# Swapping the last two block products of each fast up pair in a gated decoder block

## The chip, the cores and the metric

The kernel runs on one core of a Trainium2 chip. Its time is the device time of one execution in microseconds (us). The core has five engines with a queue of instructions each: TensorE (PE in the profile; its weight loads are listed apart as PEld), VectorE (DVE), ScalarE (ACT), GpSimd (POOL) and SyncE (SP). They work side by side and meet at semaphores. An engine takes its own instructions in the order in which they stand in its queue.

## The reference, cut to what matters

One layer of a hybrid decoder runs on 512 positions with 16 learned positions ahead of them, in float32: a normalised input goes through gated linear attention and through a pooling branch, both are merged and added to the residual, and then comes the gated MLP, where the change is. Everything is held transposed, with channels on the partitions.

```
hn = rmsnorm(h, norm2_g)
up = causal_dwconv(hn @ w_up, conv_w, conv_b)     # w_up: 1024 x 5632, conv over 3 positions
a, bv = split(up, 2)                              # 2816 channels each
h = h + (silu(a) * bv) @ w_down                   # w_down: 2816 x 1024
out = rmsnorm(h, final_norm_g)[:, 16:]
```

## The kernel before, in words

A float32 product is made of three matmuls on the format float32r: each operand is split into a high part and a remainder, and high*high, high*remainder and remainder*high are summed in PSUM.

The MLP's 2816 hidden channels are 22 tiles of 128. A step `("up", i)` makes tile i of both `a` and `bv`, so it is called a pair here; a step `("down", part, m)` makes two of the eight output tiles from a part of the hidden tiles. `seq` lists them: ups 0 to 9, two downs (n = 10, 11), up 10 (n = 12), two downs, ups 11 to 15 (n = 15 to 19), two downs, up 16 (n = 22), two downs, ups 17 to 21 (n = 25 to 29), and eight downs from n = 30. Ups 0 to 3 are done plainly by `up_plain`. The 18 ups from 4 on go through `up_fast`: the pair is seen as a product of 2x2 blocks (two halves of the contraction, two halves of the positions, `a` and `bv`), and seven block products replace eight, with sums of weight blocks and of input blocks made beforehand. Each call of `seven` is one block product: 12 matmuls of 258 columns on TensorE.

The seven products go to four PSUM banks `x`, `y`, `q` and `v`. Bank `x` gets three products on top of each other and is copied out by ScalarE after each (lines 788, 793, 797, into the blocks z11, z12 and z21 of `z`); bank `q` gets two (copied out after the first by line 790, and added to z12 by VectorE after the second, line 801); `y` and `v` get one each. A further product may only be written into a bank once the copy of its last state has been read: the fourth product waits for line 788, and the last one in `x` waits for line 793.

What each pair reads, and who makes it:

- `own[n]`, tiles `gh` and `gl` (high part and remainder of three weight blocks; two buffers each), is made by `make_own`: ScalarE writes minus the high part into `gl` (line 654), then GpSimd issues three DMAs (two for a down) that add the weights from DRAM to it (line 656), so that the remainder is left, and ScalarE copies the high part to `gh` (line 657):

```
act.activation(lo, src, AF.Copy, scale=-1.0)
for piece in pieces:
    pool.dma_start(lo[piece], dram[piece], accum_op=ALU.add)
act.activation(hi, src, AF.Copy)
```

- `sums[n]`, tiles `sh_<n>a`, `sl_<n>a`, `sh_<n>b`, `sl_<n>b` (two buffers each, shared by a and b), is made by `make_sums`: four VectorE additions within the loaded weights `raw` (line 692), in place and so only after `gh` has read them, then the two splits (ScalarE, line 249, and VectorE, line 250). The b sums of the next pair go into the buffer that this pair's b sums hold until its sixth and seventh product have read them.
- The pair ends with `prepare(n, behind)`: it fetches further weights and calls `make_own(n + 2)`, whose ScalarE instructions are queued behind the instruction `behind`, which is the copy of line 797.

After a pair, `conv` works on the pair three before it: the convolution, the gate and the split of the gated tile (lines 814 to 821, ScalarE and VectorE).

The order of the text isn't the order on an engine. The framework's scheduler gives each engine its order when the program is built: it takes what it reckons ready, by its own estimate of times. So in pair 4 TensorE runs 8 matmuls of the fifth product, all 12 of the fourth, and then the other 4 of the fifth, though the text has the fourth first. On the chip the order within an engine is fixed.

Of the kernel before, what the change touches and what calls it, by code (L numbers as in the profile page):

```python
# [13 lines left out]
ALU = mybir.AluOpType  # L14
# [54 lines left out]
def hybrid_block(ctx: ExitStack, tc: tile.TileContext, xt, g1d, wts, wup, wdown, wglr, wgk, vecs, out):  # L69
    nc = tc.nc  # L70
    act, dve, pool, pe, sp = nc.scalar, nc.vector, nc.gpsimd, nc.tensor, nc.sync
# [556 lines left out]
    def bank(name):  # L628
        return bankp.tile([P, 512], F32, tag="bank", name=name)
# [67 lines left out]
    def weights(n):  # L697
        make_sums(n)
        make_sums(n + 1)
        return (own[n], *sums.get(n, ()))  # L700

    def prepare(n, behind=None):
        fetch(n + 2)
        fetch(n + 3)
        if behind is None:
            make_own(n + 2)
        else:
            with tc.issue_after(behind.ins):
                make_own(n + 2)
# [4 lines left out]
    def pairtile(name, dt=F32):  # L714
        return flat(name, unitp, dt)
# [34 lines left out]
    direct, crossed = [], []  # L750
# [20 lines left out]
    def seven(acc, w, block, x, at, first=True):  # L771
        for k in range(4):
            for e, (a, b) in enumerate(((0, 0), (0, 1), (1, 0))):
                pe.matmul(  # L774
                    acc[:, 0:HN], w[a][:, block, k], x[k][b][:, at],
                    start=first and k == 0 and e == 0, stop=k == 3 and e == 2,
                    skip_group_check=not first,
                )

    def up_fast(n, i):  # L780
        g, sa, sb = weights(n)
        z = pairtile(f"z{i}").rearrange("p (a b) -> p a b", a=2)
        z11, z12 = (z[:, 0, a:b] for a, b in HALF)
        z21, z22 = (z[:, 1, a:b] for a, b in HALF)
        x, y, q, v_ = (bank(f"{c}{i}") for c in "xyqv")
        n_ = slice(0, HN)
        seven(x, g, 2, direct, 2)
        act.activation(z11, x[:, n_], AF.Copy)
        seven(q, sa, 0, crossed, 1)
        act.activation(z22, q[:, n_], AF.Copy)  # L790
        seven(v_, g, 0, crossed, 3)
        seven(x, sa, 1, crossed, 2, False)
        act.activation(z12, x[:, n_], AF.Copy)
        seven(y, g, 1, direct, 0)
        dve.tensor_tensor(z11, y[:, n_], z11, ALU.add)
        seven(x, sb, 1, crossed, 0, False)
        behind = act.activation(z21, x[:, n_], AF.Copy, scale=-1.0)
        dve.tensor_tensor(z22, z21, z22, ALU.subtract)
        dve.tensor_tensor(z21, v_[:, n_], z21, ALU.add)
        seven(q, sb, 0, direct, 1, False)  # L800
        dve.tensor_tensor(z12, q[:, n_], z12, ALU.add)
        prepare(n, behind)
        zs[i] = z

# [29 lines left out]
    for n, job in enumerate(seq):  # L834
        if job[0] == "up":
            i = job[1]
            (up_plain if i < PLAIN else up_fast)(n, i)
            if i >= LAG:
                conv(i - LAG)
            if i == FF - 1:  # L840
                for k in range(FF - LAG, FF):
                    conv(k)
                table(LOG_EXP, silus[-1])
        elif job[1] < 3:
            (w,) = weights(n)
            for c in range(2):
                acc = bank(f"pd{n}_{c}")
                down(acc, w, c, job[1], (0, 512))
                h = h2[2 * job[2] + c][:, META:]
                dve.tensor_tensor(h, acc, h, ALU.add)  # L850
            prepare(n)
# [113 lines left out]
```

## Time and profile before

| what | us |
|---|---|
| median of 3 runs | 855.51 |
| lowest and highest run | 855.21, 858.98 |
| the profiled execution, its own time | 854.07 |
| span of its instructions | 852.4 |

The profile is of one execution; its span leaves out 1.7 us around the program. Views used below: the page's list of busy time per engine; the waits (who waited for whom); the chain of work that ended last (each row: start, length, what; followed back from the last instruction); the timeline (start, length, engine, line, operation, out<-in, and in brackets the idle time before it with what ended it). Tile names lose their numbers in most places, so `x`, `q`, `gl`, `gh`, `raw` stand for those of all pairs; `z` of line 793 is the copy of z12, `z` of line 797 that of z21.

### The profile page before, as it was taken

How to read it: one execution, taken by the hardware profiler on the slowest of the kernel's cores; microseconds unless marked ns; L12 is line 12 of the kernel's file. 1: busy time of each engine (PE TensorE's matmuls, PEld its weight loads, DVE VectorE, ACT ScalarE, POOL GpSimd, SP SyncE). 2: the span in 40 equal slices, each digit the busy share in tenths (PEclk: the TensorE clock that was granted, in tenths of full speed). 3: DMA queues.
4: the chain of work that ended last, by engine and by line, in shares of the span. 5: the costliest groups of instructions: out<-in, count | busy, mean ns of one | idle time of the engine just before them, and what ended most of it. 6: DMA issues, size and time to landing. Idle time of an engine off the chain costs nothing.

```text
span 852.4 us, 15085 instructions
## 1 busy us (share of the span) xinstructions
PE 827.7 (97%) x6357; PEld 795.8 (93%) x6357; DVE 526.2 (62%) x817; ACT 440.4 (52%) x622; POOL 144.2 (17%) x149
## 2 busy tenths in 40 slices
PE   8999999999999999999999999999999999999993
PEld 6999999999999999999999999998899987999772
DVE  6677335379756433355555488995569844897425
ACT  7287134266234212353263357885568854777562
POOL 3000000001740000000022122221222222221241
PEclk9999999999999999999999999999999999999997
DMA  7423221122323322362275074867977777877763
GB/s 240 128 64 110 76 75 50 33 77 66 118 81 99 100 86 89 100 198 83 92 248 173 1 172 100 194 154 198 216 167 161 183 177 184 185 162 174 152 92 102
DMA packets 35780, 109.96 MB, mean 129 GB/s; under 512 B 4000, under 2 KB 6816, under 8 KB 32896
## 3 DMA queue, kind: packets, MB, share of 16 engines
q1 hardware_dynamic: 20368, 79.10, 27.8%
q0 software_dynamic: 14112, 28.84, 20.5%
q8 instruction: 50, 0.82, 0.4%
q10 hardware_dynamic: 1232, 1.05, 0.4%
q14 instruction: 18, 0.15, 0.0%
HBM read 106.88 MB, written 2.10 MB: 128 GB/s over the span
## 4 chain that ended last, share of the span: by engine, by line
PE 79%; DMA 7%; ACT 6%; DVE 5%; issue 2%; SPq 0%; DVEq 0%; POOL 0%; ACTq 0%
PE pd L829 9%; PE pu L150 5%; PE pv L150 5%; PE po L150 5%; PE pb L150 5%; PE pgb L150 5%; PE pga L150 5%; PE pr L150 5%; PE pa L150 5%; PE x L774 5%; DMA gl<-in_wdown_dram 5%; PE pup L733 4%; PE q L774 4%; PE pq L150 3%; DVE raw L692 2%
## 5 line engine op out<-in xcount | busy, mean ns | idle before, releaser
L133 ACT ACTIVATE whi<-wraw 128x1024 fp32r<-128x1024 f32 (+2 forms) x78 | 78.9, 1014 | 202.5 <-PE pa L150 36.4
L134 DVE TENSOR_TENSOR wlo<-wraw,whi 128x1024 fp32r<-128x1024 f32 (+2 forms) x78 | 94.8, 1218 | 13.0 <-ACT whi L133 7.2
L656 POOL DMA_DIRECT2D gl<-in_wup_dram x66 | 59.1, 1219 | 226.7 <-ACT gl L654 215.4
L829 PE MATMUL pd<-g,gh 128*128 128x512 f32 (+1 forms) x304 | 93.2, 388 | 0.0
L657 ACT ACTIVATE gh<-raw 128x1536 fp32r<-128x1536 f32 (+1 forms) x38 | 54.5, 1435 | 47.1 <-issue 26.1
L829 PEld LDWEIGHTS pd<-g,gh 128*128 128x128 f32 x304 | 56.5, 188 | 11.9
L829 PE MATMUL pd<-g,gl 128*128 128x512 f32 (+1 forms) x152 | 59.3, 390 | 3.2 <-DMA gl<-in_wdown_dram 3.2
L692 DVE TENSOR_TENSOR raw<-raw 128x512 f32<-128x512 f32 x72 | 49.5, 688 | 15.6 <-ACT gl L654 12.0
L654 ACT ACTIVATE gl<-raw 128x1536 fp32r<-128x1536 f32 (+1 forms) x38 | 54.4, 1431 | 0.8 <-DMA raw<-in_wup_dram 0.5
L535 POOL TENSOR_TENSOR pt<-u 128x1028 f32<-128x1028 f32 (+3 forms) x4 | 14.0, 3498 | 191.9 <-ACT whi L133 179.0
L656 POOL DMA_DIRECT2D gl<-in_wdown_dram x32 | 28.1, 1040 | 106.1 <-ACT gl L654 94.7
L850 DVE TENSOR_TENSOR h<-pd,h 128x512 f32<-128x512 f32 x24 | 16.5, 689 | 42.9 <-PE pd L829 42.8
L829 PEld LDWEIGHTS pd<-g,gl 128*128 128x128 f32 x152 | 28.6, 188 | 10.8 <-DMA gl<-in_wdown_dram 3.8
L815 DVE SCALAR_TENSOR_TENSOR cv<-z,vec,cv 128x512 f32<-128x512 f32 x44 | 32.7, 748 | 9.1 <-ACT cv L814 9.0
L814 ACT ACTIVATE cv<-z,vec 128x512 f32<-128x512 f32 x44 | 34.0, 812 | 0.0
L816 DVE SCALAR_TENSOR_TENSOR cv<-z,vec,cv 128x512 f32<-128x512 f32 x44 | 32.5, 747 | 0.2
L150 PE MATMUL pr<-xh,whi 128*128 128x258 f32 (+1 forms) x128 | 26.1, 285 | 0.0
L150 PE MATMUL pv<-xh,wlo 128*128 128x264 f32 x128 | 26.0, 285 | 0.0
L150 PE MATMUL pu<-xh,wlo 128*128 128x258 f32 (+3 forms) x128 | 25.9, 284 | 0.0
L150 PE MATMUL pv<-xl,whi 128*128 128x264 f32 x128 | 25.9, 284 | 0.0
L150 PE MATMUL pu<-xh,whi 128*128 128x258 f32 (+3 forms) x128 | 25.9, 284 | 0.0
L150 PE MATMUL pu<-xl,whi 128*128 128x258 f32 (+3 forms) x128 | 25.9, 284 | 0.0
(821 smaller groups left out, 2756.2 us busy)
## 6 DMA issues: line engine op xcount, KB each, us to landing
wraw<-in_wts_dram SPq DMA_DIRECT2D x72, 512.0 KB, 3.6
raw<-in_wup_dram SPq DMA_DIRECT2D x22, 1024.0 KB, 8.0
gl<-in_wup_dram POOLq DMA_DIRECT2D x66, 256.0 KB, 7.4
raw<-in_wdown_dram SPq DMA_DIRECT2D x12, 768.0 KB, 7.9
gl<-in_wdown_dram POOLq DMA_DIRECT2D x24, 384.0 KB, 8.1
h<-in_xt_dram SPq DMA_DIRECT2D x4, 514.0 KB, 6.0
raw<-in_wdown_dram SPq DMA_DIRECT2D x4, 512.0 KB, 4.8
gl<-in_wdown_dram POOLq DMA_DIRECT2D x8, 256.0 KB, 5.7
```

The costliest lines, as they stand in the source:

```text
L133: act.activation(hi[:, a:b], t[:, a:b], AF.Copy)
L134: dve.tensor_tensor(lo[:, a:b], t[:, a:b], f32(hi[:, a:b]), ALU.subtract)
L150: pe.matmul(acc[:, s, : b - a], w, x[:, a:b], start=(i == 0 and w is wh and x is xh), stop=(i == n - 1 and last),)
L654: act.activation(lo, src, AF.Copy, scale=-1.0)
L656: pool.dma_start(lo[piece], dram[piece], accum_op=ALU.add)
L657: act.activation(hi, src, AF.Copy)
L692: dve.tensor_tensor(raw[:, dst], raw[:, dst], raw[:, x], ALU.add)
L733: pe.matmul(acc[:, 0 : b - a], w[p], q[k][:, a:b], start=k == 0 and e == 0, stop=k == KT - 1 and e == 2,)
L774: pe.matmul(acc[:, 0:HN], w[a][:, block, k], x[k][b][:, at], start=first and k == 0 and e == 0, stop=k == 3 and e == 2, skip_group_check=n ...
L814: act.activation(cv, z[:, c, META:], AF.Identity, scale=v1("cw2", m), bias=v1("cb", m))
L815: dve.scalar_tensor_tensor(cv, z[:, c, META - 1 : L - 1], v1("cw1", m), cv, ALU.mult, ALU.add)
L829: pe.matmul(acc, w[p][:, c, k], gated[k0 + k][q][:, a:b], start=k == 0 and e == 0, stop=k == nk - 1 and e == 2,)
```

## The change

Within `up_fast` the sixth and seventh block products change places. Before, the sixth is the last one into bank `x` and the seventh the last one into bank `q`; after, `q` comes first. The VectorE addition that follows `q`'s product moves up with it. The copy of line 797, the two additions that use it, and `prepare`, whose work hangs behind that copy, keep their place behind `x`'s product and so come at the end.

```diff
         seven(y, g, 1, direct, 0)
         dve.tensor_tensor(z11, y[:, n_], z11, ALU.add)
+        seven(q, sb, 0, direct, 1, False)
+        dve.tensor_tensor(z12, q[:, n_], z12, ALU.add)
         seven(x, sb, 1, crossed, 0, False)
         behind = act.activation(z21, x[:, n_], AF.Copy, scale=-1.0)
         dve.tensor_tensor(z22, z21, z22, ALU.subtract)
         dve.tensor_tensor(z21, v_[:, n_], z21, ALU.add)
-        seven(q, sb, 0, direct, 1, False)
-        dve.tensor_tensor(z12, q[:, n_], z12, ALU.add)
         prepare(n, behind)
```

No instruction is added, removed or resized.

## The prediction

> **What bounds the kernel now.** I read the page's list of busy time first:
>
> ```profile
> span 852.4 us, 15085 instructions
> PE 827.7 (97%) x6357; PEld 795.8 (93%) x6357; DVE 526.2 (62%) x817; ACT 440.4 (52%) x622; POOL 144.2 (17%) x149
> ```
>
> TensorE is busy nearly throughout, and the change gives it the same matmuls. So it can only move the little time in which TensorE waits. The waits of TensorE and of its weight loads between 518 and 790 us come next (who waited for whom: us in total, times, longest):
>
> ```profile
> PEld pd L829 <- DMA gl<-in_wdown_dram: 3.8, 3, 2.1
> PEld x L774 <- ACT z L793: 2.7, 7, 0.4
> PE x L774 <- ACT z L793: 1.2, 6, 0.2
> ```
>
> Among the pairs one wait stands out: the sixth product, the last into bank `x`, waits for line 793's copy of z12. It happens in 7 of 18 pairs. The other row belongs to the downs. What a waiting pair costs is read from the chain of waits (start, length, what):
>
> ```profile
> 528.03 0.97 PE y L774 x8
> 529.00 1.46 PE x L774 x12
> 530.46 0.48 PE y L774 x4
> 530.93 1.72 PE x L774 x12
> ...
> 539.83 1.43 PE y L774 x12
> 541.26 1.45 PE x L774 x12
> ...
> 551.32 1.45 PE x L774 x12
> ...
> 585.46 8.29 DMA gl<-in_wdown_dram
> ...
> 593.79 7.88 PE pd L829 x33
> ...
> 636.17 1.64 PE x L774 x12
> ...
> 646.62 1.71 PE x L774 x12
> ...
> 657.14 1.73 PE x L774 x12
> ...
> 667.68 1.73 PE x L774 x12
> ...
> 733.49 1.65 PE x L774 x12
> ...
> 765.01 1.73 PE x L774 x12
> ```
>
> Without a wait a product takes 1.43 to 1.45 us, and from one sixth product to the next it is 551.32 - 541.26 = 10.06 us. With the wait it is 667.68 - 657.14 = 10.54 us. So a full wait costs 0.48 us. Six pairs have it (646.62 to 667.68, and three more, the last at 765.01). Two have a short one (636.17 and 733.49, 1.64 and 1.65 instead of 1.45: 0.2 us each), and pair 4 has 530.93 with 1.72 (0.27 us). Together 6 x 0.48 + 0.4 + 0.27 = 3.55 us.
>
> Why the copy is late stands in ScalarE's timeline of one such period:
>
> ```profile
> 655.76 1.06 ACT L249 ACTIVATE sh_18a<-raw 128x1024 fp32r<-128x1024 f32 x1 [0.84 <-DVE raw L692]
> 656.72 0.37 ACT L793 ACTIVATE z<-x 128x258 f32<-128x258 f32 x1
> 656.99 0.62 ACT L818 ACTIVATE cv<-cv 128x512 f32<-128x512 f32 x1
> 658.90 0.39 ACT L797 ACTIVATE z<-x 128x258 f32<-128x258 f32 x1 [1.29 <-PE x L774]
> 659.19 1.48 ACT L654 ACTIVATE gl<-raw 128x1536 fp32r<-128x1536 f32 x1
> 660.57 1.04 ACT L249 ACTIVATE sh_18b<-raw 128x1024 fp32r<-128x1024 f32 x1
> 661.51 1.48 ACT L657 ACTIVATE gh<-raw 128x1536 fp32r<-128x1536 f32 x1
> 662.89 0.62 ACT L249 ACTIVATE g<-cv 128x512 fp32r<-128x512 f32 x1
> 663.41 0.37 ACT L788 ACTIVATE z<-x 128x258 f32<-128x258 f32 x1
> ...
> 666.30 1.06 ACT L249 ACTIVATE sh_19a<-raw 128x1024 fp32r<-128x1024 f32 x1 [0.84 <-DVE raw L692]
> ```
>
> Line 793's copy stands behind sh_18a, and sh_18a waits for VectorE's additions in `raw`, which wait for `gh`, which stands behind sh_18b, `gl` and line 797's copy, which waits for the product that waited. That is a ring of 10.54 us, longer than TensorE's 10.06. In the earlier pairs the order is the other way round, and nothing waits:
>
> ```profile
> 559.98 0.39 ACT L793 ACTIVATE z<-x 128x258 f32<-128x258 f32 x1 [0.43 <-PE x L774]
> 561.25 1.06 ACT L249 ACTIVATE sh_8a<-raw 128x1024 fp32r<-128x1024 f32 x1 [0.88 <-DVE raw L692]
> ```
>
> **The change part by part.** Nothing is added or removed: 7 x 12 matmuls, four copies, four additions and the same DMAs per pair. The two products cost TensorE the same in either order (1.45 us each).
>
> *What goes.* Between the fourth product, which line 793 reads, and the last into `x` there is now `q`'s product as well as `y`'s. The copy has 1.45 us more, and the worst wait was 0.48. If line 793's copy is not put off by as much, all 3.55 us go.
>
> *What is moved: line 797's copy and all that hangs behind it.* It now waits for the end of the pair, 1.45 us later. Behind it on ScalarE stand `gl`, the b sums and `gh` of the rows above, and then line 788's copy for the next pair. The b sums alone lose nothing: their buffer comes free at the pair's end in both versions. I count from S, the start of the next pair's first product. A product's end in the chain lies 0.17 us after the next one's first matmul begins, and line 797's copy starts 0.03 us after that (667.68 + 1.73 = 669.41, the copy at 669.44): S + 0.20. By the rows above `gh` starts 2.61 us behind it (661.51 - 658.90), at S + 2.81, sh_a 4.79 us behind `gh` (655.76 less the `gh` of that period, one ring of 10.54 before 661.51), at S + 7.60, and line 788's copy 4.51 us behind line 797's, ending at S + 5.08. Who is late then:
>
> First, line 788's copy. The fourth product is due at S + 3 x 1.43 = S + 4.29 and needs it. It would be 0.8 us late. But the scheduler knows that, and pair 4 is the row nearest to it: there `gh` also came late, line 788's copy ran from 527.75 to 528.12, and TensorE was given 8 matmuls of `y` ahead of the fourth product and lost nothing.
>
> ```profile
> 525.86 1.47 ACT L657 ACTIVATE gh<-raw 128x1536 fp32r<-128x1536 f32 x1
> 527.24 0.61 ACT L249 ACTIVATE g<-cv 128x512 fp32r<-128x512 f32 x1
> 527.75 0.37 ACT L788 ACTIVATE z<-x 128x258 f32<-128x258 f32 x1
> ```
>
> I expect that in most pairs: with all of `y` ahead, the fourth product starts at S + 5.73 and the copy is done. The cost of an interleaved product, 1.46 instead of 1.43 (529.00), is 0.03 us x 13 pairs = 0.4 us. The bounds are 0 (an order of products without any cost) and 13 x 0.9 = 11.7 us (no reordering; 0.8 of waiting and the 0.1 that a first matmul after a wait took longer in the rows above). I take 0.4, because the only pair in this position shows it.
>
> Second, the DMAs into `gl`, issued by GpSimd after line 654. The tightest pair is number 9, whose weights are issued at 564.93 (with the landing times of its three: min, median, max); its third product reads the second of them:
>
> ```profile
> 564.93 2.65 POOL L656 DMA_DIRECT2D gl<-in_wup_dram  x3 [7.40 <-ACT gl L654]
> DMA to landing us min/median/max: 4.3/9.8/10.3
> ```
>
> ```profile
> 577.29 0.28 PE L774 MATMUL v<-xh,gl 128*128 128x258 f32 x1
> ```
>
> The second is issued at most 2.65 / 3 = 0.9 us after the first and takes at most 10.3, so it is there by 576.1, and the product that uses it starts at 577.29: 1.2 us of slack, at the worst. It turns into a wait of 0.3 us at most in this pair, and stays positive where the landing is 9.8. I take 0, with 0.3 us x 10 pairs (those whose `gl` is made two pairs earlier, within a row of pairs) = 3 us as the upper end.
>
> Third, the second down after a pair. Its `gl` is late already: pair 9's line 654 starts at 583.68, the DMA at 585.46 lands at 593.75, and the down (593.79 in the chain) waits for it.
>
> ```profile
> 583.42 0.37 ACT L797 ACTIVATE z<-x 128x258 f32<-128x258 f32 x1
> 583.68 1.48 ACT L654 ACTIVATE gl<-raw 128x1536 fp32r<-128x1536 f32 x1
> ```
>
> Line 797's copy there moves from 583.42 to the pair's end (584.24 + 0.17 = 584.4). That is 1.0 us, all on the path. The chain shows no such wait right after the pairs ending at 680 and 778, so I charge it once. Bounds: 0 and 3 x 1.45 = 4.4 us.
>
> VectorE's moved addition (line 801) costs nothing: it runs earlier, ahead of the two that wait for line 797's copy, and `conv` reads `z` three pairs later. Behind these two on VectorE stand the `raw` additions, which wait for `gh` in any case. SyncE's fetches hang on free `raw` buffers, three pairs ahead.
>
> Sum, against the profiled execution: 854.07 - 3.55 + 0.4 + 1.0 = 851.9 us. The median of the runs is 1.44 higher than that execution, so 853.4 on the scale of the runs.
>
> **The rivals.** All on the scale of the runs.
>
> *The ring stays (856.0).* If line 793's copy stays behind sh_a, it starts 0.97 us after it, at S + 8.57, and ends at S + 8.94, while the last product is due at S + 6 x 1.435 = S + 8.61: 0.33 + 0.1 = 0.43 us remain of each 0.48. What the product gains, line 797's later copy takes back. Only 0.3 + 0.65 of the 3.55 go: 854.07 - 0.95 + 1.4 + 1.44. For it speaks the order in the late pairs; against it that sh_a becomes ready 1.45 us later, so a scheduler that goes by readiness puts line 793's copy first, as at 559.98.
>
> *Line 788's copy stops the fourth product (slower, 861.5).* This is the mechanism of the first point without its rescue: in 13 pairs `gl`, the b sums and `gh`, and in most a split or a silu too, stand ahead of it. Without that last piece (0.52) the lateness is 0.45 with the restart, with it 0.9: 5.9 to 11.7 us, middle 8.5. 854.07 - 3.55 + 1.0 + 8.5 + 1.44 = 861.5. It decides once the order of the products on TensorE is left as written, or the scheduler's estimate of ScalarE is over 0.6 us too early per pair. Against it: pair 4. [...]
>
> *The change does nothing (855.5).* The scheduler could restore the order of the two products. It had no reason in the trace.
>
> *More goes than counted (850.5).* If the downs' wait for `gl` does not grow and their other waits shift favourably, another microsecond or two goes.
>
> **How the numbers follow.** Chances: forecast 0.46, ring 0.26, late line 788 0.20, nothing 0.04, more 0.04. From no change a measurement can tell about 0.5%, 4.3 us: 851.2 to 859.8. Only "more" lies below; three quarters of the late line 788's cases lie above, and some of the others' upper ends (the DMAs' 3 us): faster 0.05, same 0.77, slower 0.18. The range reaches from 851.5 to 860.5, which leaves out "more" and the upper half of the slower rival. The forecast's own range is 852 to 855.
>
> **What would show it.** In the profile after: no wait of `x` for line 793 if the first step is right, and line 793's copy ahead of sh_a; 10.06 us from pair to pair; matmuls of `y` ahead of the fourth product; line 654 right behind the pair's end; a down after pair 9 that starts 1 us later. A wait of `x` for line 788 would show the slower rival, 0.43 us for line 793 the ring, and a wait of `v` or `y` for `gl` the DMAs. I would be most wrong if the scheduler's estimate of ScalarE is off, since all the slack of line 788's copy rests on it.

## The result, and the profile after

| | median, us | runs | ratio to before (95% interval) |
|---|---|---|---|
| before | 855.77 | 855.03 to 859.78 (8) | |
| after | 862.39 | 858.44 to 865.48 (8) | 1.0062 (1.0032 to 1.0091) |

The change costs 6.6 us by the medians and 0.62% by the ratio, which would be 5.3 us; the prediction had 853.4 and a range up to 860.5. The profiled execution after is one of the longer ones (864.64 us, against 854.07 before). Three of the eight runs after lie at 858.4 to 859.3 us, with a mean granted clock of TensorE of 0.994 to 0.995, and the other five from 861.5 us on, with 0.988 to 0.991.

The first lines of the profile's page, the same ones that were shown of the kernel before:

```profile
span 862.9 us, 15104 instructions
PE 832.1 (96%) x6357; PEld 798.5 (93%) x6357; DVE 525.8 (61%) x817; ACT 440.5 (51%) x622; POOL 144.2 (17%) x149
```

The span is 10.5 us longer and TensorE shows 4.4 us more busy time with the same 6357 matmuls, so some of them took longer. The other 6 us are waits. The waits of TensorE and of its weight loads from 518 us on, after (who waited for whom: us in total, times, longest):

```profile
PE pd L829 <- DMA gl<-in_wdown_dram: 11.1, 6, 3.3
PEld pd L829 <- DMA gl<-in_wdown_dram: 10.0, 5, 3.4
PEld x L774 <- ACT z L788: 2.7, 13, 0.3
```

and the row of before that answers to the first:

```profile
PE pd L829 <- DMA gl<-in_wdown_dram: 3.2, 4, 1.7
```

In the whole view no row of `x` waiting for line 793 is left; 13 short waits for line 788 stand in its place. What grew is the downs (`pd`): 3.2 to 11.1 us of waiting for the DMAs into `gl`.

The chain of waits after shows both. First a stretch of pairs (start, length, what):

```profile
655.20 0.60 PE y L774 x5
655.81 1.65 PE x L774 x12
657.46 0.84 PE y L774 x7
658.31 1.45 PE q L774 x12
659.76 2.90 PE x L774 x24
...
666.14 1.68 PE x L774 x12
```

TensorE is given 5 matmuls of `y`, then the fourth product, then the other 7. The fourth product still waits a little (1.65 and 1.68 instead of 1.46), and the last product follows with the next pair's first in one piece, 2.90 for 24. From pair to pair it is 666.14 - 655.81 = 10.33 us, between the 10.06 of a pair without a wait and the 10.54 of a late pair before.

Then the downs, after and, in the second block, before:

```profile
576.96 8.95 DMA gl<-in_wdown_dram
...
585.96 16.14 PE pd L829 x69
...
674.55 8.79 DMA gl<-in_wdown_dram
...
683.38 16.20 PE pd L829 x69
...
702.80 10.65 DMA gl<-in_wdown_dram
...
713.50 17.89 PE pd L829 x70
...
775.48 9.30 DMA gl<-in_wdown_dram
...
784.83 7.89 PE pd L829 x33
...
794.74 1.42 ACT cv L814 x2
796.16 1.38 ACT gl L654
...
797.83 7.05 DMA gl<-in_wdown_dram
...
805.01 17.98 PE pd L829 x70
```

```profile
700.50 9.45 DMA gl<-in_wdown_dram
...
710.00 16.33 PE pd L829 x70
```

The first down after each row of pairs (n = 10, 20, 30, at 585.96, 683.38, 784.83) now waits for its `gl`; none of these three stands in the chain before. The down n = 23 waited before too, but less. And the 70 matmuls behind the two longest waits (n = 23 and 32) take 17.9 to 18.0 us instead of 16.3.

To put a size on each part I took the start-to-start distances of neighbouring matmuls from 505 us on, less the usual one (0.12 us in the pairs, 0.23 in the downs):

| lost time of TensorE, us | before | after |
|---|---|---|
| waits in the pairs | 3.7 | 3.7 |
| waits in the downs | 4.9 | 13.2 |
| of these n = 10, 20, 30 | 0, 0, 0 | 1.3, 1.2, 1.7 |
| n = 11 | 0.8 | 0 |
| n = 13, 23 | 0.4, 1.9 | 1.4, 3.2 |
| n = 32 | 0.8 | 3.4 |
| n = 35 and 37 together | 1.0 | 1.0 |
| matmuls spaced too widely in the downs | 0.7 | 4.0 |

8.3 us of waits and 3.3 us of spacing make 11.6. The profiled execution of after reaches its first fast pair 1.5 us earlier (522.11 against 523.56 us), so 10.1 of the 10.5 us are accounted for.

**Why the DMAs into `gl` land later.** For the down n = 10, GpSimd's and SyncE's timelines around line 654, and the landing times (min, median, max) of its two DMAs; first before, then after:

```profile
574.99 1.75 POOL L656 DMA_DIRECT2D gl<-in_wdown_dram  x2 [7.41 <-ACT gl L654]
576.92 0.33 SPq L646 DMA_DIRECT2D raw<-in_wup_dram  x1
DMA to landing us min/median/max: 4.9/7.7/10.5
```

```profile
576.31 0.33 SPq L646 DMA_DIRECT2D raw<-in_wup_dram  x1
576.96 1.75 POOL L656 DMA_DIRECT2D gl<-in_wdown_dram  x2 [7.76 <-ACT gl L654]
DMA to landing us min/median/max: 9.0/9.7/10.5
```

SyncE's fetch of the next weights (1 MB into `raw`) comes nearly at its old place. Line 654 comes 2 us later, and so its DMAs have passed from ahead of the fetch to behind it. The first piece, which the down reads first, then takes 9.0 us instead of 4.9. The down started at 584.24 before, 4.3 us after that piece had landed; now the piece lands at 585.91. Two microseconds in the queue became six at the landing. At n = 20 it is 5.2 and 8.8.

Two microseconds are more than the 1.45 of the moved product. ScalarE's timeline shows the rest, before and then after (line 799 is line 797 of before):

```profile
572.93 0.39 ACT L797 ACTIVATE z<-x 128x258 f32<-128x258 f32 x1
573.21 1.48 ACT L654 ACTIVATE gl<-raw 128x1536 fp32r<-128x1536 f32 x1
574.59 1.05 ACT L249 ACTIVATE sh_9b<-raw 128x1024 fp32r<-128x1024 f32 x1
```

```profile
573.96 1.06 ACT L249 ACTIVATE sh_9b<-raw 128x1024 fp32r<-128x1024 f32 x1 [0.49 <-PE x L774]
574.93 0.37 ACT L799 ACTIVATE z<-x 128x258 f32<-128x258 f32 x1
575.19 1.48 ACT L654 ACTIVATE gl<-raw 128x1536 fp32r<-128x1536 f32 x1
```

The scheduler has put the split of the b sums ahead of the copy and of line 654, where it stood behind them before. This puts line 654 off by 0.97 us more. It also brings the fetch forward: the fetch waits for VectorE's half of the same split, which reads `raw` last (it ends at 576.90 before and at 576.28 after, and the fetch follows at 576.92 and 576.31). So the two passed each other from both sides. What the old order on ScalarE would have saved by itself was not tried.

This covers the 4.2 us of n = 10, 20 and 30. The `gl` of n = 13 and 23 stands 0.27 us behind a fetch in both kernels and is issued nearly as long ahead of its down as before (6.9 and 7.1 us against 6.9 and 7.2); its landing took 1.0 and 1.2 us longer (7.67 to 8.69, 9.45 to 10.65), and this trace doesn't show why.

Theory G: the loss is `gl` being late for the downs. Theory D, its cause: the fetch just ahead of it. Rival P: the pairs themselves (the 13 waits for line 788, the split order of products). "The early hook" below means that `make_own` is queued behind line 793's copy instead of line 797's.

### The profile page after: what moved, and what is told of

Read it like the earlier page. It is cut to its first block, busy times and chain, and to the rows that moved or that the text cites. A ratio compares the mean times of both kernels' runs of the same rounds, so it can differ in the third digit from the quotient of the medians.

```text
span 862.9 us, 15104 instructions
## 1 busy us (share of the span) xinstructions
PE 832.1 (96%) x6357; PEld 798.5 (93%) x6357; DVE 525.8 (61%) x817; ACT 440.5 (51%) x622; POOL 144.2 (17%) x149
## 4 chain that ended last, share of the span: by engine, by line
PE 85%; DMA 7%; ACT 3%; issue 2%; DVE 2%; SPq 0%; DVEq 0%; ACTq 0%
PE pd L829 11%; DMA gl<-in_wdown_dram 7%; PE x L774 6%; PE pu L150 5%; PE pv L150 5%; PE po L150 5%; PE pb L150 5%; PE pup L733 5%; PE pgb L150 5%; PE pga L150 5%; PE pr L150 5%; PE pa L150 5%; PE q L774 4%; PE pq L150 3%; PE y L774 2%
## 5 line engine op out<-in xcount | busy, mean ns | idle before, releaser
L829 PE MATMUL pd<-g,gh 128*128 128x512 f32 (+1 forms) x304 | 95.2, 395 | 0.0
L829 PE MATMUL pd<-g,gl 128*128 128x512 f32 (+1 forms) x152 | 61.0, 401 | 11.1 <-DMA gl<-in_wdown_dram 11.1
```

The source lines that it names most:

```text
L829: pe.matmul(acc, w[p][:, c, k], gated[k0 + k][q][:, a:b], start=k == 0 and e == 0, stop=k == nk - 1 and e == 2,)
```

## The experiments

| | order | hook | fetch | median, us | ratio to before (95%) | waits in pairs / downs / wide spacing, us |
|---|---|---|---|---|---|---|
| before | old | late | SyncE | 855.77 | | 3.7 / 4.9 / 0.7 |
| after | swapped | late | SyncE | 862.39 | 1.0062 (1.0032 to 1.0091) | 3.7 / 13.2 / 4.0 |
| e1 | swapped | early | SyncE | 851.79 | 0.9954 (0.9931 to 0.9978) | 0.2 / 5.3 / 0.8 |
| e2 | old | later still | SyncE | 860.15 | 1.0050 (1.0023 to 1.0077) | 3.2 / 8.8 / 0.7 |
| e3 | swapped, 10 pairs | late | SyncE | 860.91 | 1.0060 (1.0035 to 1.0085) | 2.7 / 12.7 / 7.0 |
| e4 | swapped, 8 pairs | late | SyncE | 861.39 | 1.0066 (1.0043 to 1.0090) | 3.5 / 12.2 / 2.5 |
| e5 | old | early | SyncE | 852.87 | 0.9966 (0.9946 to 0.9987) | 2.3 / 4.4 / 2.1 |
| e6 | swapped | late | behind gl | 849.23 | 0.9924 (0.9898 to 0.9949) | 3.6 / 3.1 / 0.5 |
| e7 | swapped | early in 8 pairs | SyncE | 856.24 | 1.0008 (0.9984 to 1.0032) | 2.9 / 9.0 / 3.8 |
| e8 | swapped | early | behind gl | 842.47 | 0.9845 (0.9820 to 0.9869) | 0.0 / 0.9 / 0.3 |
| e9 | old | late | behind gl | 846.08 | 0.9887 (0.9862 to 0.9913) | 3.5 / 1.1 / 0.3 |
| e10 | old | early | behind gl | 844.51 | 0.9871 (0.9843 to 0.9899) | 2.0 / 1.0 / 0.3 |

Each group of experiments had its own executions of before (medians 854.89 to 856.02 us), and each ratio is against those. The last column is from the one profiled execution. e2's was the shortest of its 12 (856.77 us) and e3's the longest (865.66); e7's took 859.81.

**e1: the swap with `make_own` hooked early.**

```diff
-        act.activation(z12, x[:, n_], AF.Copy)
+        behind = act.activation(z12, x[:, n_], AF.Copy)
...
-        behind = act.activation(z21, x[:, n_], AF.Copy, scale=-1.0)
+        act.activation(z21, x[:, n_], AF.Copy, scale=-1.0)
```

> The new order of products, but make_own(n + 2) is queued behind line 793's copy (z12, the fourth product) instead of the copy at the pair's end. Theory G (late gl: line 654 starts behind the pair's end, its DMAs land late, and the downs wait for them): the downs' waits for gl fall from 13 us in the profile to the 5 us of before or less, no TensorE clock under 1.00 in the down stages, 852 to 855 us, ratio to before 0.996 to 1.000. Rival P (the order of the products itself costs: waits of the fourth product for line 788, other use of banks and of VectorE): it stays over 858 us.

851.79 us, just below the expected range. The swapped order stays, and the whole loss is gone. The waits of TensorE in the downs from 518 us on:

```profile
PE pd L829 <- DMA gl<-in_wdown_dram: 3.7, 2, 2.2
PEld pd L829 <- DMA gl<-in_wdown_dram: 3.2, 2, 2.7
```

No wait for line 788 or 793 is left in that view, and the matmuls of the downs wait twice for the DMA instead of six times. This points to what hangs behind line 797's copy, not to the order of products. (The early hook mends the pairs too, so e1 alone does not weigh G against P; e6 does.)

**e2: the old order, with a late hook.** A copy of one column of `q` at the pair's end, with `make_own` behind it:

```diff
+        behind = act.activation(mark, q[:, 0:1], AF.Copy)
         prepare(n, behind)
```

> The old order of products, plus a one-column copy by ScalarE of q at the pair's end, and make_own(n + 2) is queued behind that. Theory G: gl is late without any change in the products, so the loss is there: 858 to 864 us, with downs that wait for gl at n = 10, 20 and 30. Rival P: 855 to 856.5 us (18 tiny copies, at most 0.3 us each off TensorE's path).

860.15 us, a ratio of 1.0050 where the swap has 1.0062: most of the loss without any swap (18 small copies are in it as well). The downs' waits grow from 4.9 to 8.8 us, those of the pairs do not. But the waits aren't where they were expected: n = 10 and 20 wait not at all and n = 30 for 0.4 us. Line 654 comes later here than after the swap (577.48 against 575.19 us), and the fetch went out 2.7 us ahead of `gl`, whose first piece lands in 5.2 us. The downs that wait are n = 13, 23 and 33 (1.8, 2.5 and 2.4 us). So e2 shows that a late hook costs by itself, and not that it costs in the way that the swap does at n = 10, 20 and 30.

**e3 and e4: the swap in one part of the pairs only.** In the 10 pairs whose `prepare` makes `gl` for another pair (e3), or in the 8 that make it for a down (e4):

```diff
+        if seq[n + 2][0] == "up":        # e4: "down"
+            ...                          # the sixth and seventh swapped
+        else:
+            ...                          # as before
```

> The products trade places only in the 10 pairs whose prepare makes the weights of another pair; the 8 pairs whose prepare makes the weights of a down keep the old order. Theory G: the downs' waits are those of before (5 us) and the time is 853 to 857 us. Rival P: 10 of 18 pairs carry the loss, 858 to 861 us.

> The complement: the products trade places only in the 8 pairs whose prepare makes the weights of a down. Theory G: the downs wait for gl as in the changed kernel (10 to 13 us), 857 to 863 us. Rival P: 8 of 18 pairs carry the loss, 857 to 859 us, without longer waits in the downs.

e4 is as expected: 8 pairs alone bring the whole loss (861.39). e3 is a miss: 860.91, in the range that P had, though the waits in its pairs are shorter than before (2.7 us). As G says, n = 10 doesn't wait (its `gl` DMA goes out at 574.12, ahead of the fetch at 576.05), but other downs do. The chain of e3:

```profile
603.10 10.95 DMA gl<-in_wdown_dram
...
614.09 17.79 PE pd L837 x70
...
703.14 10.63 DMA gl<-in_wdown_dram
...
713.82 19.04 PE pd L837 x70
```

n = 13 and 23 wait 3.6 and 3.3 us for DMAs that take 10.6 to 11.0. Their `gl` is made by a down, not by a pair, and stands behind a fetch in every kernel with the fetch on SyncE; before, these landed in 7.67 (n = 13) and 9.45. The two edits together cost less than the sum of each. At n = 13 of e3 both the down and its `gl` come 2.2 us earlier than after the swap, and the landing takes 10.95 instead of 8.69 us; why it does is open. So "the pair in front is at fault" was too narrow; the fetch is common to all.

**e5: the old order with the early hook.**

> The old order of products with make_own(n + 2) queued behind line 793's copy (z12) instead of line 797's. It tells what of the first experiment's gain is the earlier gl and what is the swap. If the place of gl is all that matters, it runs like the swapped kernel with the early hook, 851 to 853 us. If the swap is worth the waits for line 793 that it takes away (3.5 us), those waits stay here or grow, and it runs at 854 to 857 us.

852.87 us. The swap is worth 1.1 us with the early hook (851.79), inside the intervals, and costs 6.6 with the late one.

**e6: the swap, with the fetch queued behind `gl`.** Line 654 keeps its late place. The fetch of step n + 4 goes from SyncE to GpSimd's queue, behind the DMAs into `gl`:

```diff
...
-            pool.dma_start(lo[piece], dram[piece], accum_op=ALU.add)
+            added.append(pool.dma_start(lo[piece], dram[piece], accum_op=ALU.add))
...
             with tc.issue_after(behind.ins):
                 make_own(n + 2)
+        with tc.issue_after(added[-1].ins):
+            fetch(n + 4, pool)
```

> The changed kernel, but the weights of step n + 4 are fetched by GpSimd's queue right behind the DMAs into gl of step n + 2, so that a fetch never stands ahead of gl's DMAs (before, SyncE issued it when a buffer came free). Theory D (gl is late by 2 us and then lands later too, because the fetch of 1 MB now stands ahead of it: 9 us instead of 5): first pieces of gl land within 4 to 6 us, the downs wait 5 us or less in the profile, 853 to 857 us. Rival L (line 654's later start alone makes the waits): the downs still wait 8 us or more, 858 to 863 us.

849.23 us, better than the expected 853 to 857, and the clearest run for D. The same stretch of GpSimd's timeline, the landing, and then the chain:

```profile
576.80 1.74 POOL L658 DMA_DIRECT2D gl<-in_wdown_dram  x2 [7.22 <-ACT gl L656]
577.89 1.20 POOL L646 DMA_DIRECT2D raw<-in_wup_dram  x1
DMA to landing us min/median/max: 5.0/5.9/6.9
```

```profile
584.24 16.55 PE pd L833 x72
...
610.85 16.55 PE pd L833 x72
...
786.80 5.53 DMA gl<-in_wdown_dram
```

(Line 658 here is 656 of before.) `gl` is issued within 0.2 us of the swapped kernel's time, yet its first piece lands in 5.0 us instead of 9.0. Eight downs run in four unbroken pieces of 72 matmuls, of which the first two are shown; n = 32 still waits most (1.9 us). Meanwhile the waits in the pairs are as after (3.6): the rival of late starts alone (L), which needs 8 us or more of waits in the downs, falls, and so does rival P, since the waits for line 788 are there and the kernel is 13 us faster. Two things limit what e6 says. The edit changes the fetch's queue as well as its place, so it doesn't say which of the two did it. And 1.7 of the 13 us have nothing to do with `gl`: in the four kernels with the fetch on GpSimd, the stretch from the start of the downs' last matmul to the end of the span is 12.9 to 13.1 us instead of 14.8. Why is not known.

**e7: the swap, with the early hook in the 8 pairs ahead of downs.**

> The changed kernel, with the early hook (behind line 793's copy) only in the 8 pairs whose prepare makes the weights of a down; the other 10 keep the hook at the pair's end. Theory G: the downs no longer wait more than before, only the waits of the fourth product for line 788 stay (3.5 us): 854 to 857 us. If the waits at the later downs (n = 13, 23 and 32), which stayed when those 8 pairs kept the old order, come from something other than these pairs' gl, it stays at 858 to 861 us.

856.24 us, in theory G's range: by the median the loss is gone (ratio 1.0008, 0.9984 to 1.0032), though not the 3 us that e1 gained on before. Theory G's reason holds in part only. n = 10, 20 and 30 lose their waits, but in the profiled execution the downs still wait 9.0 us, where 5 were expected: n = 13 and 23 wait 3.2 and 2.9 us, as in e3. Moving single `gl`s does not undo the late landings of the others (10.50 and 10.45 us at n = 13 and 23).

**e8: both edits on the swap.**

> Both remedies with the swap: early hook, and the fetch behind gl's DMAs on GpSimd's queue. Theory D: the waits that the early hook left at n = 13, 23 and 32 (0.3, 2.4 and 1.6 us) shrink, 848 to 851.5 us. If those waits have nothing to do with a fetch ahead of gl: 851 to 853 us.

842.47 us (842.38 to 842.84), the best of all, better than both kernels and than the range of either expectation. No wait in the pairs, and 0.9 us in the downs: the chain has the four downs from n = 30 on in one piece.

```profile
769.59 33.08 PE pd L833 x143
```

**e9 and e10: is the swap worth anything then?** The old order with the fetch behind `gl`, and with both edits.

> The order before the change, with the fetch of the weights of step n + 4 issued by GpSimd behind the additions into gl(n + 2). What is open is whether the swap itself is worth its waits once no fetch stands ahead of gl. Theory V, the swap is worth what its own stages say (pair waits 3.7 us before, 3.6 us in the changed order, because the new waits for line 788's copy took the place of those for line 793's): this kernel is within 1 us of the same edit on the changed order (849.2), 848 to 851, pair waits about 3.7, down waits about 3. Theory W, the swap still costs by its later line 654 even so: 845 to 847, down waits under 2. Theory X, the swap gains 3.5 us: 852 to 854.

> The order before the change with both edits: make_own queued behind line 793's copy, and the fetch behind the additions into gl. With the swap these two gave 842.5, with no wait left in the pairs. Theory V: in the old order the two edits leave about 2.3 us of pair waits, since line 793's copy, on which make_own now hangs, has only one product between it and the product that waits; 844 to 846, down waits about 1. Theory W: 841 to 842.5, equal or better than with the swap. Theory X: 846 to 848.

846.08 and 844.51 us. e9 falls in W's range and outside V's: with the hook late, the swap costs 3 us even with the fetch out of the way (849.23, though the two intervals overlap a little). In the profiles most of that is the tail: from n = 30 on 73.7 us in e6 and 71.4 in e9, where n = 32 does not wait. e10 falls in V's range: with both edits the swap gains 2.0 us (842.47). There the waits of the weight loads for line 793's copy (797 in these kernels) remain in the old order, from e9 to e10:

```profile
PEld x L778 <- ACT z L797: 2.7, 7, 0.4
```

```profile
PEld x L778 <- ACT z L797: 0.6, 2, 0.4
```

By matmul distances, with the 0.1 us that each restart takes (behind the matmul that waited at 657.14 of before, the next one starts after 0.22 us instead of 0.12), 2.0 us of pair waits stay in e10 and none in e8. That is the swap's gain. It is real (the executions of the two kernels lie apart, though the intervals of the ratios overlap), and it is little more than half of the 3.55 us that I had credited, and to be had in full only with two other edits.

## Why the prediction was wrong, point by point

- **What goes: right as a mechanism, its value taken back.** All the waits for line 793 went, as forecast, and line 793's copy is no longer late. The 3.55 us did go.
- **First, line 788's copy: the cost of 0.4 us was mis-sized.** The rescue came (`y` ahead of the fourth product), but not fully. 13 pairs still wait 0.2 us for line 788, some 0.3 us with the restart. That makes 3.7 us instead of 0.4, and the time lost to waits in the pairs is 3.7 us in both kernels: they neither gain nor lose. Pair 4, from which I took the price, had 8 matmuls of `y` ahead, and I expected all 12; nine of the pairs after have 5, and eight have none. The bounds of 0 and 11.7 held it. The rival "Line 788's copy stops the fourth product" came near the result (861.5) with a mechanism that accounts for 3.7 us, as much as the swap gained, and not for the loss.
- **Second, the DMAs into `gl`, taken at 0: this step failed.** I looked at the tightest pair and let the landing stay at its old 4.3 to 10.3 us. No pair waited for `gl`, but the transfer itself changed when its issue passed the fetch: 4.9 to 9.0 us. I wrote that SyncE's fetches "hang on free `raw` buffers, three pairs ahead", which is why they did not move along; I never asked what line 654 would move past on the other queue. I also took over ScalarE's old order, `gl` and then the b sums. After the swap the b split stands first, line 797's copy starts at S + 1.10 instead of S + 0.20 (574.93, with the next pair's start at 573.83), and the fetch hangs on that split.
- **Third, the second down after a pair, 1.0 us: this step failed too.** I charged the down that was late already (n = 11) and no other, as the chain showed no wait for the first downs. Their slack was 4.1 to 4.3 us, and it went: 1.3 + 1.2 + 1.7 us at n = 10, 20, 30. n = 11's own 0.8 vanished: its `gl` is issued 1.2 us later than before, but lands in 4.7 us instead of 8.3. The waits at n = 13, 23 and 32 grew by 1.0, 1.3 and 2.6. Together 8.3 us against 1.0, and above the bound of 4.4.
- **Not in the prediction: TensorE's clock.** 3.3 us of wide spacing behind the two longest waits, with a granted clock of 0.83 in each of the stretches 709.8 to 720 and 802 to 812 us (the last section shows the first).

Worked again with what the runs showed: 854.07 - 3.7 (line 793, by the distances) + 3.7 (line 788) + 8.3 (downs) + 3.3 (spacing) - 1.5 (ahead of the pairs) = 864.2; the profiled execution took 864.64.

What stays open: the landings at n = 13 and 23 vary from 7.6 to 11.0 us between kernels that all have a fetch just ahead, and I did not settle by what. At n = 32, a split and the convolution's first step (line 814, twice) stand ahead of line 654 on ScalarE after the swap, as the chain shows; that order was not tried by itself. And no run moved the fetch behind `gl` on SyncE's own queue, so for n = 13 and 23 the place of the fetch and its queue are not told apart.

## What to carry to other kernels

When an edit moves the instruction behind which a DMA is issued, read the new order on that engine, which the scheduler sets afresh, and list what the other queues issue in the same few microseconds: at n = 10 the move itself was 2.0 us, and with the 1 MB fetch 0.65 us ahead of it the first piece took 4.0 us more to land (8.95 instead of 4.94). A transfer that lands ahead of its use shows up nowhere in the waits (4.1 to 4.3 us ahead at n = 10, 20 and 30 of before), so compute its slack before calling it free. And judge a reordering with the resource that hides it out of the way: this swap cost 6.6 or 3.1 us, or brought 1.1 or 2.0 us, according to the place of two other things.

## What the hardware showed beyond that

**TensorE kept to the order of its queue.** At 657.14 of before it idles 0.21 us until line 793's copy is done, although `q`'s product, next in its queue, had all it reads: its bank had been copied out by 653.51 (line 790) and its b sums were made by 652.32. Up to the point where the two kernels part, the two profiled executions have the same order on each engine: the first 4357 of 6357 matmuls on TensorE, 353 of 622 instructions on ScalarE, 476 of 817 on VectorE, and all 149 on GpSimd, at times that differ by up to 1.5 us (GpSimd by up to 10.8).

**The landing went with the order of issue, and not with it alone.** The first piece of `gl` (384 KB) for the first down after a row of pairs (n = 10, 20, 30) landed in 4.8 to 5.2 us where SyncE's next fetch (1 MB; 768 KB at n = 30) went out 1.1 to 2.1 us later (before, e1, e3, and n = 20 and 30 of e5 and e7), in 7.9 to 9.3 where it went out 0.3 to 0.7 us earlier (after, e4, and n = 10 of e5 and e7), and in 4.8 to 5.2 again where it went out 2.6 to 2.7 us earlier (e2). The order of these two is not all. For the second down n = 11 of before the next fetch went out 1.1 us later, and the piece took 8.29 us; two earlier fetches were on their way (issued at 576.92 and 577.35, landed at 586.22 and 587.87, with the piece issued at 585.46). In the four kernels with the fetch on GpSimd's queue, the first pieces for n = 10 to 33 landed in 4.6 to 6.9 us, also with a fetch on its way.

**Behind some waits the matmuls ran slower.** TensorE's timeline behind the wait of n = 23, after and then before:

```profile
714.94 0.63 PE L829 MATMUL pd<-g,gl 128*128 128x512 f32 x1
715.37 1.06 PE L829 MATMUL pd<-g,gh 128*128 128x512 f32 x2
```

```profile
710.78 0.39 PE L829 MATMUL pd<-g,gl 128*128 128x512 f32 x1
711.01 0.62 PE L829 MATMUL pd<-g,gh 128*128 128x512 f32 x2
```

A matmul follows the one ahead of it after 0.43 us (714.94 to 715.37) instead of 0.23 (710.78 to 711.01), for about eight matmuls, which costs 1.6 us. The granted clock of after (PEclk, third from the end) is lower there, 0.83, with the stretch behind it at 1.00 for comparison:

```profile
709.80:720.00 10.20, 7.18 (x26) 5.48 (x25) 1.55 (x3) 3.13 (x3) 1.75 (x2) 0.83 0.95 225
720.00:731.20 11.20, 11.20 (x50) 9.19 (x49) 5.95 (x8) 4.99 (x4) 2.64 (x3) 1.00 0.35 58
```

Over the twelve profiles, this followed 9 of the 15 gaps of 2.3 us and more ahead of a down's `gl` (from the start of one matmul to the start of the next), and none of the 14 gaps of 1.0 to 2.2 us. It cost 1.5 to 1.7 us in seven of the nine, and 2.3 and 2.8 in two of e3. It did not go by length alone: gaps of 2.32, 2.41 and 2.75 us were followed by it and one of 3.67 was not (2.41 and 3.67 both in e4). What decided isn't shown, nor whether the same kernel meets it in one execution and not in another: the granted clocks of the eight runs after, from 0.988 to 0.995, would fit that, but only one of them has a profile.
